# Full-height second score products in a three-layer fp32 network: 64-row matmuls replaced by 128-row ones over twice-stored low parts

## The chip, the cores and the metric

The kernel runs on one core of one Trainium2 chip. The metric is the device time of one execution in microseconds (us), lower is better. The engines are PE (TensorE, matmul; its weight loads are listed apart as PEld), DVE (VectorE), ACT (ScalarE), POOL (GpSimd) and SP (SyncE, whose queue issues nearly all DMAs).

## The reference

One sequence of 512 tokens with 1024 channels goes through three layers and a last norm, in float32:

```
layer 1: x += norm(w_out(gated sum of three mixers)):  gated linear attention (4 heads),
         sliding-window attention (8 heads of 64, 2 key heads), multi-scale pooling;  then a conv-FFN
layer 2: x += fox(x):   16 heads of 64;  scores q.k/8 plus a forgetting bias, causal softmax;  then a conv-FFN
layer 3: x += mla(x):   16 heads;  scores (q_nope.k_nope + q_rope.k_rope) / sqrt(192), 128 and 64 rows;
         the rotary key k_rope is one for all heads;  block-causal softmax;  then a conv-FFN
out = norm(x)
```

What matters here are the scores: products over 64 rows (the head's channels) in the sliding-window heads, in all fox heads, and in the rotary part of every mla head.

## The kernel before

**Two-part products.** To keep float32 accuracy with single-pass matmuls, every operand is kept as a pair of fp32r parts, a high and a low one. A product of two pairs is three matmuls into one PSUM bank (`mm3`): high by high, high by low, low by high. The large projections stream their weights from HBM (`raw` chunks of 512 KB on SP's queue, split into `hi` by ACT, L276, and `lo` by DVE, L277) and run with 512 token columns.

**Scores of 64-row heads.** Two heads with 64 rows each share a tile of 128 rows. `stack_q` (L423) makes a tile `Q` whose plane j holds, for head j, its high part in one half of the 128 rows and its low part in the other. `stack_k` (L432) makes `K`, whose plane j holds head j's high part twice, in both halves: ACT casts the key tile to `KH` (L437), four SBUF-to-SBUF DMAs on SP's queue (L440, 64 rows by 512 columns each, two per head) copy it, and DVE subtracts the rest to `KL` (L441), which stays where it is, one head in rows 0 to 63 and the other in rows 64 to 127. A score tile is then two matmuls (`mm_stacked`, L444): `Q` by `K` over all 128 rows, which gives (high + low of q) by (high of k), and a second one over the 64 rows of the head alone, high of q by low of k. In the profile these are `sc<-K,Q` and `sc<-KL,Q`, in the sliding-window part `swas<-K,Q` and `swas<-KL,Q`.

**Rotary part.** In `mla` the rotary key `kr` already stands in both halves of the rows, as a high and a low tile. A score tile there is three 128-row matmuls (`sc<-hl`), then `qr` by `kr[0]` over 128 rows, then `qr` by `kr[1]` over 64 rows (both are `sc<-hl,Q`).

**Each head** takes its four query blocks one after the other, with 128, 256, 384 and 512 key columns (sliding window: 128 and three times 256), two matmuls each (five in mla). So the matmuls of a head are a burst in which the 128-row and the 64-row form alternate. After the burst come the row maxima (DVE), exponentials (ACT), normalisation (ACT and POOL), ten transposes on PE (`t<-cst,pa` and the like), their split into `pth` (ACT) and `ptl` (DVE), and the product with the values (`fpo`, `mpo`).

**Order.** PE's order is fixed by the program. A head is a task whose steps go between the matmuls of the projections: after each step it says how many us of PE work, by a table of costs, are to pass before the next one (`LAG`; for example 22.08 between a fox head's scores and its transposes), and `mm` advances that clock by a cost per column that knows nothing of rows. The other engines' order is made by a list scheduler. All tiles come out of pools with a fixed number of buffers: `nslot` = 36 slots of 4 KB per partition, 9 of 2 KB (`t2`), 8 PSUM banks. In `fox` a pair of heads is begun by the projections `fq` and `fk`, `stack_q` and `stack_k`; there are eight pairs. The sliding-window part calls `stack_k` once.

Of the kernel before, what the change touches and what calls it, by code (L numbers as in the profile page):

```python
# [7 lines left out]
F32 = mybir.dt.float32  # L8
# [10 lines left out]
UPC = 8        # 128x128 units in one chunk of the weight stream  # L19
# [4 lines left out]
WHOLE = (6, 8, 7)     # output tiles that are not computed by halves of the tokens  # L24
LEVELS = (64, 32, 16, 8, 4, 2, 1)

# columns of the parameter array
# [12 lines left out]
# columns of the constant array  # L40
# [6 lines left out]
# columns of the array of narrow weights, and how many for each k  # L47
_NCOLS = {"glow": (0, 32), "fgt": (256, 32), "krope": (512, 64)}
NRES = 384     # columns that stay on chip
# [5 lines left out]
def tfk_plan():  # L55
    """The weight stream: one entry for each 128x128 unit, in the order of use."""
    plan = []

    def cols(name, k0, nk, c0, nn=1):
        while len(plan) % nn:  # L60
            plan.append(None)
        for k in range(nk):
            for n in range(nn):
                plan.append((name, k0 + k, c0 + n))

    for k in range(8):
        for n, t in FIRST:
            plan.append((n, k, t))
    cols("gv", 0, 8, 0, 4)
    cols("sv", 0, 8, 0)  # L70
    cols("sk", 0, 8, 0)
    for t in range(4):
        cols("sq", 0, 8, t)
    for t in range(4):
        cols("pu", 0, 8, t)
    for t in range(4):
        cols("gr", 0, 8, t)
    cols("poolw", 0, 4, 0)
    for br in "cba":
        for t in range(8):  # L80
            cols("gate_" + br, 0, 8, t)
            cols("br_" + br, 0, 4, t)
    def align():
        while len(plan) % UPC:
            plan.append(None)

    def grouped(name, k0, nk, tiles):
        for k in range(nk):
            for t in tiles:
                plan.append((name, k0 + k, t))  # L90

    grouped("wout", 0, 8, range(WOUT_WHOLE))
    align()
    for t in range(WOUT_WHOLE, 8):
        cols("wout", 0, 8, t)

    def ffn(i):
        tiles = [j * DFF_T + t for t in range(DFF_T) for j in range(2)]
        if i == 0:
            align()  # L100
            grouped("up0", 0, 8, tiles[:UP0_FIRST])
            tiles = tiles[UP0_FIRST:]
        for t in tiles:
            cols(f"up{i}", 0, 8, t)
        whole = WHOLE[i]
        for t in range(whole):
            cols(f"down{i}", 0, DFF_T, t)
        for _ in range(2):
            for t in range(whole, 8):
                cols(f"down{i}", 0, DFF_T, t)  # L110

    ffn(0)
    cols("fv", 0, 8, 0, 4)
    align()
    cols("fq", 0, 8, 0)
    cols("fv", 0, 8, 0, 4)
    cols("fv", 0, 8, 4, 4)
    for p in range(8):
        if p:
            cols("fq", 0, 8, p)  # L120
        cols("fk", 0, 8, p)
    grouped("fout", 0, 8, range(4))
    for t in range(4, 8):
        cols("fout", 0, 8, t)
    ffn(1)
    for t in range(2):
        cols("dkv", 0, 8, t)
    for t in range(6):
        cols("dq", 0, 8, t)

    def mout(g):
        for t in range(8):
            cols("mout", 4 * g, 4, t)

    def keys_values(p):
        for h in (2 * p, 2 * p + 1):
            cols("uk", 0, 2, h)
        for g in UV_AT.get(p, ()):
            cols("uv", 0, 2, 4 * g, 4)

    for p in range(8):
        if p == 0:
            keys_values(p)
        for t in (0, 2, 1):
            cols("uq", 0, 6, 3 * p + t)
        if p:
            keys_values(p)
        if p in MOUT_AFTER:
            mout(MOUT_AFTER[p])
    mout(3)  # L150
    ffn(2)
    align()
    return plan


def tfk_kept(e):
    """Whether the unit stays on chip for a second use."""
    return e and (e[0] == "wout" and e[2] >= WOUT_WHOLE or e[0] == "up0" and (e[2] % DFF_T) * 2 < UP0_FIRST
                  or e[0] == "fq" and e[2] == 0)
# [6 lines left out]
# the work of TensorE that goes between a step of a task and the next one, which needs its result  # L166
# [10 lines left out]
class Fut:  # L177
    """A value that a task in the background will set."""
# [17 lines left out]
class Net:  # L196
    def __init__(self, ctx, tc, xin, wall, par, cst, msk, nar, out, dbg=None):
# [8 lines left out]
        self.nslot, self.nt2 = 36, 9  # L206
# [29 lines left out]
    # ---- allocation  # L236
# [27 lines left out]
    # ---- the weight stream  # L264
# [33 lines left out]
    def narrow(self, name):  # L298
        """The weights of a product of few columns, by k: [high, low] of w columns each, as one operand."""
        nc, (c, w) = self.nc, _NCOLS[name]  # L300
        raw = self.slot([P, 8, w], F32, "nraw")
        hl = self.slot([P, 8, 2, w], F32R, "nhl")
        nc.sync.dma_start(out=raw, in_=self.nar[:, c:c + 8 * w].rearrange("p (k w) -> p k w", k=8))
        nc.scalar.copy(out=hl[:, :, 0], in_=raw)
        nc.vector.tensor_tensor(out=hl[:, :, 1], in0=raw, in1=hl[:, :, 0].bitcast(F32), op=ALU.subtract)
        return [hl[:, k].rearrange("p a w -> p (a w)") for k in range(8)]

    # ---- tasks whose products go between those of the projections
# [28 lines left out]
    # ---- products  # L337
# [14 lines left out]
    def proj(self, name, t, xs, k0=0, ps=None, cols=ALL):  # L352
        """out^T tile t of the product with the moving operands xs (pairs of high and low parts)."""
# [8 lines left out]
    def proj_narrow(self, ws, xs, ps=None, cols=ALL):  # L362
        """Two passes: the product has its parts in the rows from 0 and from w on."""
# [7 lines left out]
    def add_narrow(self, ps, w, n):  # L371
        """The sum of the parts of such a product, n rows of it."""
# [15 lines left out]
    def proj_halves(self, tiles, halves):  # L388
        """As proj_group, for moving operands whose halves of the tokens come one after the other."""
# [5 lines left out]
    def proj_tok(self, name, c0, xs, ms=range(4), pss=None):  # L395
        """Token-major product: tiles of [128 tokens, 512 columns]."""
# [13 lines left out]
    # ---- splitting  # L410
# [4 lines left out]
    def split_scaled(self, src, scale, out=None):  # L415
        """src * scale in two parts; scale is a number or a column."""
# [6 lines left out]
    def stack_q(self, q):  # L423
        """[[high; low], [low; high]] of two heads of 64 rows."""
# [7 lines left out]
    def stack_k(self, k):  # L432
        """[[high; high], [high; high]] of two heads of 64 rows, and [low; low] of both."""
        nc = self.nc
        K = self.slot([P, 2, T], F32R, "K")
        H, L = (self.t2(dt=F32R, name=n) for n in ("KH", "KL"))
        nc.scalar.copy(out=H, in_=k)  # L437
        for j in range(2):
            for r in range(2):
                nc.sync.dma_start(out=K[64 * r:64 * r + 64, j].bitcast(F32), in_=H[64 * j:64 * j + 64].bitcast(F32))  # L440
        nc.vector.tensor_tensor(out=L, in0=k, in1=H.bitcast(F32), op=ALU.subtract)  # L441
        return K, L

    def mm_stacked(self, out, Q, K, L, j, qs, ks, start=True):  # L444
        r = slice(64 * j, 64 * j + 64)
        self.mm(out, Q[:, j, qs], K[:, j, ks], start, False)
        self.mm(out, Q[r, j, qs], L[r, ks], False, True)
# [8 lines left out]
    # ---- norms  # L456
    def rsqrt(self, src, inv_d, w):
        """(src * inv_d + EPS) ** -0.5 for [128, w]"""
# [20 lines left out]
    def bcast(self, rs):  # L479
        """[128, n] by token -> PSUM [128, 128 n], the same in each partition."""  # L480
# [15 lines left out]
    def add_square(self, acc, src, eng=None, cols=ALL, first=False):  # L496
        """acc += src * src, in the given columns"""
# [23 lines left out]
    def x_start(self, nxt):  # L521
        """x gets new values; nxt names the gain that its next use has."""
# [6 lines left out]
    def x_ready(self, k, cols=ALL):  # L529
        """x tile k has its values in these columns: what the next part needs of it."""  # L530
# [24 lines left out]
    def normed(self, gain):  # L555
        """The parts of x * gain; the factor by token comes later, from stats."""
        return [self.split_scaled(self.xk(k), self.p(gain, k)) for k in range(8)]

    def log_sigmoid(self, z, b, shape, out):
        """out = log_sigmoid(z + b), z in PSUM or SBUF, b a column."""  # L560
# [13 lines left out]
    # ---- first layer  # L574
    def mixer(self, nxt):
# [13 lines left out]
        # gated linear attention  # L589
# [24 lines left out]
        # sliding window attention  # L614
# [18 lines left out]
        # pooling  # L633
# [168 lines left out]
    def swa(self, t, g, q, k, V, of, fut):  # L802
        """Head t + 4 g."""
# [87 lines left out]
    def post_norm(self, name, xs, gain, nxt, group, whole):  # L891
        """x += rmsnorm(product) * gain; the tiles from `whole` on go by halves of the tokens, so that
        the norm of the first half runs beside the products of the second."""
# [55 lines left out]
    def finish(self, h, sq):  # L949
        """The last norm, of half of the tokens."""  # L950
# [15 lines left out]
    # ---- feed-forward  # L966
# [30 lines left out]
    # ---- causal softmax attention, shared parts  # L997
    def soft(self, src, dst, mx):
        """dst[n] = softmax of src[n] along the keys."""
# [21 lines left out]
    def transpose_probs(self, p):  # L1021
        """[(high, low)] of the transposed weights by key block: [128 keys, 512 - 128 kb queries]"""
# [13 lines left out]
    # ---- forgetting attention  # L1036
    def fox(self, nxt):
# [33 lines left out]
        def bias(h):  # L1071
            """-cum of the keys, the same for each query, and with the mask of the block on the diagonal."""
# [53 lines left out]
    # ---- latent attention  # L1126
    def mla(self, nxt):
# [28 lines left out]
        def rope(src, scl, stack):  # L1156
            """[128, 512] of rows x1 x2 x1 x2 (32 each), src in PSUM or SBUF"""
# [24 lines left out]
        def head(h, qn, kn, qr, V, fut):  # L1182
            j = h % 2
            r = slice(64 * j, 64 * j + 64)
            sc = self.score_bank()
            mx = self.tiny([P, 4], F32, "mx")
            for n in range(4):
# [3 lines left out]
                self.mm(sc[n], qr[r, j, n * P:w], kr[1][r, 0:w], False, True)  # L1191
# [89 lines left out]
# ---- layout on the host  # L1281
# [106 lines left out]
```

## Time and profile before

| | |
|---|---|
| three runs | 2290.30, 2292.85, 2297.34 us; median 2292.85 |
| profiled execution, first to last instruction (span) | 2290.4 us, 2.4 us under the median |
| PE busy | 2254.1 us, 98% |
| DVE, ACT, POOL busy | 62%, 45%, 12% |
| DMA | 206.30 MB; q1, which SP feeds, 28.5% of the 16 engines |
| PE's share of the chain that ended last | 91% |

A span is the time between the first and the last instruction of the program; busy shares are averages over stages with different limits. PE's matmuls overlap each other and their ends are modelled, so a PE that is busy all the time need not be at its full rate: what one matmul costs is read from where the next one starts.

### The profile page before, as it was taken

The numbers are of one execution on the slowest core, as the hardware profiler recorded it, in microseconds if no ns is written. First come the engines' busy times: TensorE is split into PE (matmuls) and PEld (weight loads), VectorE is DVE, ScalarE is ACT, GpSimd is POOL, SyncE is SP. The second block draws the span as 40 slices with busy tenths as digits, with TensorE's granted clock in tenths as the row PEclk, the third lists the DMA queues.
The fourth block names the chain that finished last, engine by engine and source line by source line (L and its number), as shares of the span: only waits on it lengthen the run. The fifth ranks groups of instructions, "written<-read, shape, count | busy, mean of one in ns | idle before, by whom it ended". The sixth has DMA issues, their size and how long they took to land.

```text
span 2290.4 us, 27755 instructions
## 1 busy us (share of the span) xinstructions
PE 2254.1 (98%) x10664; PEld 1850.6 (81%) x10664; DVE 1421.2 (62%) x2349; ACT 1021.8 (45%) x1672; POOL 278.7 (12%) x231
## 2 busy tenths in 40 slices
PE   8999999999999998999999999999999999999998
PEld 6777888898888897777888888887788788888887
DVE  6778544578777248667677774357555556777623
ACT  4343322354444235566544443235645564444322
POOL 4211100030000004454200000002100101000000
PEclk9989999999999999999999999999999999999998
DMA  4200323332332343433233333332122212233323
GB/s 159 65 28 28 101 93 101 101 102 74 93 101 94 99 129 122 125 98 102 65 92 98 95 100 94 101 100 71 47 65 65 74 47 92 92 102 92 101 94 100
DMA packets 61956, 206.30 MB, mean 90 GB/s; under 512 B 7152, under 2 KB 9584, under 8 KB 61824
## 3 DMA queue, kind: packets, MB, share of 16 engines
q1 hardware_dynamic: 61392, 203.74, 28.5%
q8 instruction: 84, 1.38, 0.2%
q10 hardware_dynamic: 432, 0.79, 0.1%
q14 instruction: 48, 0.39, 0.1%
HBM read 197.65 MB, written 2.13 MB: 87 GB/s over the span
## 4 chain that ended last, share of the span: by engine, by line
PE 91%; DVE 5%; ACT 1%; issue 1%; DMA 1%; POOL 0%; SPq 0%; DVEq 0%; ACTq 0%; POOLq 0%
PE up L339 31%; PE down L339 14%; PE sc L339 5%; PE uq L339 4%; PE mout L339 4%; PE gate_a L339 2%; PE gate_b L339 2%; PE gate_c L339 2%; PE fq L339 2%; PE fout L339 2%; PE wout L339 2%; PE lev L339 2%; PE fk L339 2%; PE sq L339 1%; DVE xs L420 1%; PE mpo L339 1%
## 5 line engine op out<-in xcount | busy, mean ns | idle before, releaser
L277 DVE TENSOR_TENSOR lo<-raw,hi 128x1024 fp32r<-128x1024 f32 (+1 forms) x348 | 440.4, 1266 | 325.0 <-ACT hi L276 320.7
L339 PE MATMUL up<-xs,hi 128*128 128x512 f32 x2016 | 621.7, 390 | 0.0
L276 ACT CAST hi<-raw 128x1024 fp32r<-128x1024 f32 (+1 forms) x348 | 365.4, 1050 | 571.7 <-PE down L339 171.1
L339 PEld LDWEIGHTS up<-xs,hi 128*128 128x128 f32 x2016 | 378.2, 188 | 79.4 <-issue 1.0
L339 PE MATMUL up<-xs,lo 128*128 128x512 f32 x1008 | 392.2, 389 | 0.0
L339 PE MATMUL down<-hl,hi 128*128 128x512 f32 (+1 forms) x1188 | 332.7, 366 | 0.0
L339 PEld LDWEIGHTS down<-hl,hi 128*128 128x128 f32 x1188 | 214.8, 189 | 36.3
L339 PEld LDWEIGHTS up<-xs,lo 128*128 128x128 f32 x1008 | 189.2, 188 | 39.3
L339 PE MATMUL down<-hl,lo 128*128 128x512 f32 (+1 forms) x594 | 217.1, 365 | 0.0
L502 POOL TENSOR_TENSOR acc<-acc,sq 128x256 f32<-128x256 f32 (+1 forms) x48 | 56.2, 1170 | 771.3 <-ACT sq L499 769.7
L979 DVE TENSOR_TENSOR u<-up,rsb 128x512 f32<-128x512 f32 x132 | 90.2, 687 | 80.9 <-PE up L339 76.7
L981 ACT ACTIVATE c<-u,par 128x512 f32<-128x512 f32 x132 | 107.0, 814 | 60.1 <-DVE u L979 59.8
L339 PEld LDWEIGHTS down<-hl,lo 128*128 128x128 f32 x594 | 112.0, 189 | 18.0
L982 DVE SCALAR_TENSOR_TENSOR c<-u,par,c 128x511 f32<-128x511 f32 x132 | 98.5, 747 | 23.8 <-ACT c L981 23.7
L918 POOL TENSOR_TENSOR x<-x,yo 128x256 f32<-128x256 f32 x32 | 28.7, 933 | 608.6 <-DVE yo L917 608.6
L983 DVE SCALAR_TENSOR_TENSOR c<-u,par,c 128x510 f32<-128x510 f32 x132 | 98.9, 749 | 4.0
L339 PE MATMUL uq<-hl,hi 128*128 128x512 f32 x288 | 90.5, 395 | 1.4 <-POOL hl L453 1.4
L452 ACT CAST hl<-c 128x512 fp32r<-128x512 f32 x66 | 40.8, 618 | 104.6 <-DVE c L990 104.6
L339 PE MATMUL mout<-hl,hi 128*128 128x512 f32 x256 | 80.4, 395 | 0.0
L988 ACT ACTIVATE c<-c 128x512 f32<-128x512 f32 x66 | 41.6, 630 | 70.1 <-DVE c L983 70.0
L420 DVE SCALAR_TENSOR_TENSOR xs<-x,par,xs 128x512 fp32r<-128x512 f32 (+1 forms) x64 | 61.9, 1006 | 7.9 <-ACT xs L419 7.9
L339 PEld LDWEIGHTS uq<-hl,hi 128*128 128x128 f32 x288 | 53.2, 188 | 14.9 <-issue 2.2
(392 smaller groups left out, 3995.1 us busy)
## 6 DMA issues: line engine op xcount, KB each, us to landing
raw<-in_wall_dram SPq DMA_DIRECT2D x359, 512.0 KB, 3.5
K<-KH SPq DMA_DIRECT2D x36, 128.0 KB, 2.3
bias<-cumd SPq DMA_DIRECT2D x16, 256.0 KB, 4.0
out_dram<-x SPq DMA_DIRECT2D x8, 256.0 KB, 2.4
x<-in_x_dram SPq DMA_DIRECT2D x7, 256.0 KB, 5.4
raw<-in_wall_dram SPq DMA_DIRECT2D x2, 256.0 KB, 4.0
early<-in_cst_dram SPq DMA_DIRECT2D x1, 512.0 KB, 6.3
msk<-in_msk_dram SPq DMA_DIRECT2D x1, 512.0 KB, 6.5
```

The lines of the kernel that those rows point to most:

```text
L276: nc.scalar.copy(out=hi[:, c], in_=raw[:, c])
L277: nc.vector.tensor_tensor(out=lo[:, c], in0=raw[:, c], in1=hi[:, c].bitcast(F32), op=ALU.subtract)
L339: self.nc.tensor.matmul(out, lhsT=a, rhs=b, start=start, stop=stop)
L420: nc.vector.scalar_tensor_tensor(out=lo, in0=src, scalar=scale, in1=hi.bitcast(F32), op0=ALU.mult, op1=ALU.subtract)
L452: nc.scalar.copy(out=hi, in_=src)
L502: (eng or self.nc.vector).tensor_tensor(out=acc[:, cols], in0=acc[:, cols], in1=sq[:, cols], op=ALU.add)
L918: nc.gpsimd.tensor_tensor(out=x, in0=x, in1=yt, op=ALU.add)
L979: v.tensor_tensor(out=u, in0=ps, in1=rsb, op=ALU.mult)
L981: nc.scalar.activation(out=c, in_=u, func=AF.Identity, scale=self.p(conv, 88 + t), bias=self.p(conv, 132 + t))
L982: v.scalar_tensor_tensor(out=c[:, 1:], in0=u[:, 0:T - 1], scalar=self.p(conv, 44 + t), in1=c[:, 1:], op0=ALU.mult, op1=ALU.add)
L983: v.scalar_tensor_tensor(out=c[:, 2:], in0=u[:, 0:T - 2], scalar=self.p(conv, t), in1=c[:, 2:], op0=ALU.mult, op1=ALU.add)
L988: nc.scalar.activation(out=g, in_=g, func=func)
```

## The change

The second matmul of a score tile now spans all 128 rows. For this `stack_k` makes a second slot tile `L`, in which plane j holds head j's low part in both halves, by four more DMAs; so `Q` by `L` also adds the product of the two low parts, which was left out before. In `mla` the row slice is dropped from `qr` and `kr[1]`, whose rows stand there twice already. The slots go from 36 to 39; a parameter that reserves memory for DMA descriptors of the program is set to 1024 so that they fit. Comments and doc strings that the diff removes are left out here.

```diff
-        self.nslot, self.nt2 = 36, 9
+        self.nslot, self.nt2 = 39, 9
...
     def stack_k(self, k):
         nc = self.nc
-        K = self.slot([P, 2, T], F32R, "K")
-        H, L = (self.t2(dt=F32R, name=n) for n in ("KH", "KL"))
-        nc.scalar.copy(out=H, in_=k)
-        for j in range(2):
-            for r in range(2):
-                nc.sync.dma_start(out=K[64 * r:64 * r + 64, j].bitcast(F32), in_=H[64 * j:64 * j + 64].bitcast(F32))
-        nc.vector.tensor_tensor(out=L, in0=k, in1=H.bitcast(F32), op=ALU.subtract)
+        out = K, L = [self.slot([P, 2, T], F32R, n) for n in ("K", "L")]
+        parts = [self.t2(dt=F32R, name=n) for n in ("KH", "KL")]
+        nc.scalar.copy(out=parts[0], in_=k)
+        nc.vector.tensor_tensor(out=parts[1], in0=k, in1=parts[0].bitcast(F32), op=ALU.subtract)
+        for a, b in zip(out, parts):
+            for j in range(2):
+                for r in range(2):
+                    nc.sync.dma_start(out=a[64 * r:64 * r + 64, j].bitcast(F32), in_=b[64 * j:64 * j + 64].bitcast(F32))
         return K, L
 
-    def mm_stacked(self, out, Q, K, L, j, qs, ks, start=True):
-        r = slice(64 * j, 64 * j + 64)
-        self.mm(out, Q[:, j, qs], K[:, j, ks], start, False)
-        self.mm(out, Q[r, j, qs], L[r, ks], False, True)
+    def mm_stacked(self, out, Q, K, L, j, qs, ks):
+        self.mm(out, Q[:, j, qs], K[:, j, ks], True, False)
+        self.mm(out, Q[:, j, qs], L[:, j, ks], False, True)
...
             j = h % 2
-            r = slice(64 * j, 64 * j + 64)
...
                 self.mm(sc[n], qr[:, j, n * P:w], kr[0][:, 0:w], False, False)
-                self.mm(sc[n], qr[r, j, n * P:w], kr[1][r, 0:w], False, True)
+                self.mm(sc[n], qr[:, j, n * P:w], kr[1][:, 0:w], False, True)
...
-    nc = _bacc.Bacc("TRN2", target_bir_lowering=False, num_devices=1)
+    nc = _bacc.Bacc("TRN2", target_bir_lowering=False, num_devices=1, dynamic_dma_scratch_size=1024)
```

On PE, in the sliding-window part, the score burst of a head reads as follows (`swas` is the PSUM bank of the scores; the sizes are those of the output):

```order
 L339 MATMUL swas<-K,Q 128x128
-L339 MATMUL swas<-KL,Q 128x128
+L339 MATMUL swas<-L,Q 128x128
 L339 MATMUL swas<-K,Q 128x256
-L339 MATMUL swas<-KL,Q 128x256
+L339 MATMUL swas<-L,Q 128x256
 L339 MATMUL swas<-K,Q 128x256
-L339 MATMUL swas<-KL,Q 128x256
+L339 MATMUL swas<-L,Q 128x256
```

Nothing moves on PE, here and in the whole program: the same matmuls stand in the same places, and the second of each pair takes another tile.

On SP's queue, in `fox`, from the third pair of heads to the fifth, there stood (`raw` is the weight stream, `bias` a copy for the forgetting bias):

```order
L440 DMA K<-KH 64x512 x4
L1074 DMA bias<-cumd 128x512 x2
L275 DMA raw<-in_wall_dram 128x1024 x2
L440 DMA K<-KH 64x512 x4
L1074 DMA bias<-cumd 128x512 x2
L275 DMA raw<-in_wall_dram 128x1024 x2
L440 DMA K<-KH 64x512 x4
```

and now there stands:

```order
L442 DMA K<-KH 64x512 x4
L442 DMA L<-KL 64x512 x4
L1075 DMA bias<-cumd 128x512 x2
L275 DMA raw<-in_wall_dram 128x1024 x2
L442 DMA K<-KH 64x512 x4
L275 DMA raw<-in_wall_dram 128x1024
L442 DMA L<-KL 64x512 x4
L1075 DMA bias<-cumd 128x512 x2
L275 DMA raw<-in_wall_dram 128x1024
L442 DMA K<-KH 64x512 x4
L442 DMA L<-KL 64x512 x4
```

Four issues more for each pair, behind those of `K`; in the fourth pair a transfer of the weight stream has come between the two.

On ACT, in `fox`, ahead of the fifth pair's key cast, there stood (`pa` holds a head's probabilities, `pts` the split of its transposes):

```order
L276 CAST hi<-raw 128x1024
L437 CAST KH<-fk 128x512
L1010 ACTIVATE pa<-pa,den 128x128
L1010 ACTIVATE pa<-pa,den 128x384
L452 CAST pts<-t_8135 128x256
```

and now there stands:

```order
L276 CAST hi<-raw 128x1024
L1011 ACTIVATE pa<-pa,den 128x128
L1011 ACTIVATE pa<-pa,den 128x384
L437 CAST KH<-fk 128x512
L453 CAST pts<-t_8165 128x256
```

In this pair the cast that `K`'s copies wait for stands behind two normalisations. Outside `fox`, and one place in the sliding-window part, the other engines' orders are as before.

## Rows read from the trace of the kernel before

**Rows 1.** The page: PE's busy time; the chain that ended last, by engine.

```profile
PE 2254.1 (98%) x10664; PEld 1850.6 (81%) x10664; DVE 1421.2 (62%) x2349; ACT 1021.8 (45%) x1672; POOL 278.7 (12%) x231
...
PE 91%; DVE 5%; ACT 1%; issue 1%; DMA 1%; POOL 0%; SPq 0%; DVEq 0%; ACTq 0%; POOLq 0%
```

**Rows 2.** Timeline of PE, a fox head's scores: start us, us, instruction.

```profile
942.66 0.39 PE L339 MATMUL fk<-xs,lo 128*128 128x512 f32 x1
942.89 0.22 PE L339 MATMUL sc<-K,Q 128*128 128x128 f32 x1
943.04 0.33 PE L339 MATMUL sc<-KL,Q 64*128 64x128 f32 x1
943.29 0.38 PE L339 MATMUL sc<-K,Q 128*128 128x256 f32 x1
...
945.51 0.73 PE L339 MATMUL fk<-xs,hi 128*128 128x512 f32 x2
946.08 0.40 PE L339 MATMUL fk<-xs,lo 128*128 128x512 f32 x1
```

**Rows 3.** Timeline of PEld (weight loads), the same burst.

```profile
942.66 0.19 PEld L339 LDWEIGHTS sc<-K,Q 128*128 128x128 f32 x1
943.03 0.18 PEld L339 LDWEIGHTS sc<-KL,Q 64*128 64x128 f32 x1 [0.18 <-issue]
```

**Rows 4.** Timeline of PE, an mla head's scores.

```profile
1590.47 0.44 PE L339 MATMUL sc<-hl 128*128 128x128 f32 x3
1590.76 0.53 PE L339 MATMUL sc<-hl,Q 128*128 128x128 f32 x2
...
1595.02 0.73 PE L339 MATMUL uq<-hl,hi 128*128 128x512 f32 x2
1595.59 0.39 PE L339 MATMUL uq<-hl,lo 128*128 128x512 f32 x1
```

**Rows 5.** Timeline of PE, a fox head's product with the values.

```profile
1016.12 0.34 PE L339 MATMUL fpo<-pth,fV 128*128 128x384 f32 x1
1016.30 0.35 PE L339 MATMUL fpo<-ptl,fV 128*128 128x384 f32 x1
1016.49 0.40 PE L339 MATMUL fpo<-pts,fV 128*128 128x256 f32 x2
1016.72 0.22 PE L339 MATMUL fpo<-pth,fV 128*128 128x128 f32 x1
```

**Rows 6.** Timeline of PE, first and next row of a sliding-window head's burst.

```profile
109.12 0.33 PE L339 MATMUL swas<-K,Q 128*128 128x128 f32 x1
...
111.50 1.22 PE L339 MATMUL sq<-xs,hi 128*128 128x512 f32 x2
```

**Rows 7.** Timelines of ACT, SP and PE: key copies, first and last fox pair.

```profile
937.02 0.61 ACT L437 CAST KH<-fk 128x512 fp32r<-128x512 f32 x1
937.66 2.38 SPq L440 DMA_DIRECT2D K<-KH  x4
...
1080.86 0.61 ACT L437 CAST KH<-fk 128x512 fp32r<-128x512 f32 x1
1084.45 0.30 PE L339 MATMUL sc<-K,Q 128*128 128x128 f32 x1 [1.43 <-DVE ptl L453]
```

**Rows 8.** The page's DMA issues: count, KB each, median us to landing.

```profile
K<-KH SPq DMA_DIRECT2D x36, 128.0 KB, 2.3
```

**Rows 9.** Windows: us, busy us by engine, PE's granted clock, DMA share, GB/s.

```profile
118.30:132.00 13.70, 13.70 (x42) 10.44 (x43) 8.38 (x21) 5.29 (x13) 2.87 (x2) 0.50 0.00 0
1087.70:1091.10 3.40, 3.40 (x12) 2.96 (x11) 1.80 (x10) 1.70 (x6) 0.00 (x0) 0.50 0.00 0
940.00:1100.00 160.00, 157.71 (x713) 118.61 (x712) 108.39 (x348) 102.98 (x251) 77.93 (x59) 0.99 0.34 99
1590.00:1880.00 290.00, 290.00 (x1403) 232.59 (x1402) 158.38 (x325) 171.57 (x366) 29.67 (x23) 1.00 0.19 60
```

**Rows 10.** Waits of PE from 940 to 1100 us: total, times, longest.

```profile
PE fpo L339 <- DVE ptl L453: 0.9, 3, 0.4
```

## The prediction

> **What bounds the kernel now.** I read the page first: PE is busy for 98% of the span and holds 91% of the chain that ended last [rows 1], so time is won or lost where PE's next matmul starts earlier or later. A busy PE is no PE at its rate, so the second view is the timeline of PE through the scores of one head of each kind, where the distance from one start to the next is read, not the duration. What a matmul of full height costs stands beside it: 0.23 us with 512 columns (`fk` to the first `sc`) [rows 2], 0.18 with 384 and 0.115 with 256 [rows 5], 0.10 with 128 (three in 0.29) [rows 4].
>
> In a fox head's burst the starts are further apart than that. `K,Q` with 128 columns is followed after 0.15, and the 64-row one after it by the next full one after 0.25 us, though 0.10 of streaming is due. The loads show why: the first load of the burst starts 0.23 us ahead of its matmul, while the one before runs; the load for the 64-row matmul starts with its matmul, after 0.18 us in which PEld waited for nothing that the profile shows [rows 3]. At each change of height PE runs empty first. DVE, ACT and DMA are not what bounds these stretches now: from 940 to 1100 us DVE is busy 108.39 and ACT 102.98 of 160, in mla 158.38 and 171.57 of 290 [rows 9].
>
> **What it removes.** The eight fox products take 942.89 to 945.51, 2.62 us [rows 2]. At full height throughout they take two each of 0.10, 0.115, 0.18 and 0.23, that is 1.25: 1.37 less. The two `fk` after the burst take 0.57 where 0.46 is due [rows 2]; with that 0.11 a head saves 1.48, and 16 heads 23.7 us.
>
> An mla head's twenty products take 1590.47 to 1595.02, 4.55 us; five of each size at full rate are 3.13; with the same 0.11 after it (two `uq` in 0.57) a head saves 1.53 [rows 4], and 16 heads 24.6 us. Here the full-height form of this very operand is in the trace: `qr` by `kr[0]` follows `sc<-hl` without a gap, the 64-row one is what follows it.
>
> A sliding-window head takes 109.12 to 111.50, 2.38 us [rows 6]; two of 0.10 and six of 0.115 are 0.89: 1.49 each, 11.9 us for eight. The step behind the burst I leave out: some bursts stand beside 64-row products of the linear attention, where a change remains.
>
> Removed in sum: 23.7 + 24.6 + 11.9 = **60.2 us** of PE time, all of it on the chain. No product is added, moved or made wider, and a product of full height takes as long as its columns.
>
> **What it adds.** 36 more copies of 128 KB on SP's queue. Four issues take 2.38 us, 0.60 each [rows 7], and a copy lands 2.3 us after its issue [rows 8]. A first head needs plane 0 of `L`: issues five and six. So `L` is there 5 x 0.60 + 2.3 = 5.3 us after the first issue of `K`, which follows `KH`'s end at once (937.63, 937.66) [rows 7]; before, `KL` was ready with DVE's subtraction.
> - First pair: 937.66 + 5.3 = 942.96, and the second product is due at 942.89 + 0.10 [rows 2]: on time.
> - Last pair: `KH` ends at 1081.47, `L` lands at 1086.8, the product is due at 1084.55: 2.25 late. This pair shows the wait already: its first product waits 1.43 us [rows 7]. The profile names DVE, but `K`'s second copy lands at 1081.5 + 0.6 + 2.3 = 1084.4, so I take it for the copy.
> - The distance from `KH`'s end to the scores is 5.26 us in the first and 2.98 in the last pair. Between the two ends I take the mean, 1.13 us for each of eight: **9 us**, bounds 0 (all like the first) and 18 (all like the last; the pair whose `KH` now stands behind two normalisations, and the one with a `raw` transfer ahead of `L`, lean there). Second heads come later and lose nothing. The sliding-window part makes one `L`, and between its key projection and its first scores PE runs the 24 products of `sq`, 24 x 0.23 = 5.5 us, which covers the copies; if not, it costs 5.3 us once.
> - Behind `L` on SP stand `bias` and `raw`, 2.4 us later each pair. A pair takes some 20 us (160 by eight) [rows 9], of which `K` and `L` take 4.8 on SP, so the queue has room; were that cover gone, the `raw` delay would be PE's, 2.4 x 8 = 19 us, inside the next bound.
>
> The other cost is on the queues of DVE and ACT. In fox PE comes back to a head's value product when `ptl` is ready, and three times it waited already, 0.9 us in all [rows 10]. Heads without slack give back what their burst saves. Below, nothing; above, all of fox's 23.7. With three such heads shown I take four: 4 x 1.5 = **6 us**. In mla PE is busy for all 290.00 us, and DVE and ACT for under 60% [rows 9]; shortened by 24.6 of 290 they stay under 65%, so I count nothing.
>
> The DVE subtraction, the cast and the operand `Q` are as before. Three more slots issue nothing; `L` is held by them. The reserved memory is that of descriptors, and the program's DMAs stay on the same queues: nothing.
>
> **Sum.** 60.2 - 9 - 6 = 45 us. On the profiled span 2290.4 - 45 = 2245; on the median of the runs, 2.4 us above it, **2248 us**.
>
> **A rule that speaks against it.** In the trace a full-height load runs while a full-height matmul does: the load at 942.66 starts with `fk`, 0.23 us ahead of its product [rows 2, 3], and three full products of 128 columns follow each other in 0.29 [rows 4] though one load takes 0.19. The Trainium skill, "TensorE: Matmul & The Clock Gate", section on packing small matmuls, says that a weight load overlaps a running matmul only when their row groups differ. By that rule full-height products would each show their load. The trace does not agree, and I follow it.
>
> **Rivals.**
> - *Loads no longer hidden.* If the 160 second products each showed their 0.19 us load, 30 us of the 60 would be gone: 2248 + 30 = 2278. Against it: `sc<-hl` in rows 4. Chance 0.02.
> - *Fox becomes bound by DVE, ACT and the copies.* PE's fox stretch would shrink from 160 to 136 us, with DVE's 108 and POOL's 78 and chains between them. With both costs at their upper bounds, 18 + 23.7, time is 2293 - 60 + 41 = 2274. For it: the waits of rows 7 and 10 exist. Against it: most value products had no wait. Chance 0.16.
> - *The clock.* From 118.30 to 132.00 PE was granted 0.50, that is 1.2 in place of 2.4 GHz, in the sliding-window part, where the bursts stand; so also for 3.4 us from 1087.70, some 3 us behind the last fox pair's wait and scores [rows 7, 9]. A denser burst could spare the first: half of 13.7, 6.9 us, time 2241 (0.10). Waits of 2 us for `L` in every pair could bring the second eight times: 8 x 1.7, time 2262 (0.10).
> - *Slower.* `L` comes so late that its wait exceeds what the kernel saves: eight pairs would each have to wait 60/8 = 7.5 us. The place is SP's queue, where `L` stands behind a `raw` that waits for its buffer; but that order is in one pair of eight, and 2.25 us is what the last pair shows. At 9 us a pair: 2293 - 60 + 72 = 2305. Chance 0.02.
> - *It does nothing*, if the empty time came from the change of operand and not of height: 2293. Against it: `sc<-hl` to `hl,Q` at full height shows none. Chance 0.02.
>
> **How the numbers follow.** The forecast has 0.58, with a range of its own from 2238 (both costs a third) to 2257. The range for 8 in 10 goes from 2233 (no cost at all) to 2266, which leaves out about half of the fox rival, the small ones and some of the clock on either side. A difference under 0.3%, 7 us, is about what a measurement of this kernel cannot tell from none; faster by more than that 0.96, within 0.02, slower 0.02.
>
> **What would show it.** Right: in mla the burst takes 3.1 to 3.3 us in place of 4.55 and the stretch is 23 to 25 us shorter; in fox a burst whose `L` is there takes 1.3; a sliding-window burst 0.9. The copy: PE waits ahead of the second score product of fox's later pairs, 1 to 2.5 us. Wrong: starts in a burst that stay 0.2 us apart beyond their columns; PE waits for `pth`, `ptl` or PSUM in most fox heads; waits in mla; or half-clock stretches behind the new waits.

## The result and the profile after

| | before | after |
|---|---|---|
| runs, us | 2289.21 to 2297.34, median 2291.57 (4) | 2253.37 to 2258.01, median 2254.90 (4) |
| profiled span, us | 2290.4 | 2251.7 |

The ratio is 0.9838, with a 95% interval from 0.9815 to 0.9861: 36.7 us less, where the forecast was 45. The time lies in the range from 2233 to 2266, and under the 2274 of the rival in which fox is bound elsewhere; by stage the picture is another one, as the windows below show.

The page of the changed kernel, the two lines that answer to [rows 1]:

```profile
PE 2196.6 (98%) x10664; PEld 1837.5 (82%) x10664; DVE 1415.0 (63%) x2349; ACT 1020.5 (45%) x1672; POOL 279.2 (12%) x231
...
PE 85%; DVE 8%; ACT 3%; DMA 2%; issue 2%; SPq 1%; POOL 0%; DVEq 0%; ACTq 0%; POOLq 0%
```

PE executes the same 10664 matmuls in 57.5 us less busy time, but the span fell only by 38.7: the chain now runs through DVE, ACT and DMA for 13% in place of 7%.

Where the time went is read by stage. Each row is one window: us, then busy us (and count) of PE, PEld, DVE, ACT, POOL, then PE's mean granted clock, DMA share and GB/s. The first is the sliding-window part (first `swas` to last `pu`), the second fox (first `sc` to last `fout`), the third mla (first `sc` to last `mpo`). Before:

```profile
109.10:225.10 116.00, 115.79 (x553) 89.84 (x553) 88.82 (x224) 48.52 (x123) 19.11 (x17) 0.90 0.09 28
942.90:1144.20 201.30, 198.69 (x915) 152.70 (x914) 137.02 (x383) 124.74 (x287) 89.54 (x66) 0.99 0.32 93
1590.50:1885.40 294.90, 294.90 (x1429) 236.86 (x1427) 161.07 (x328) 172.71 (x368) 29.17 (x23) 1.00 0.19 58
```

After:

```profile
108.90:206.60 97.70, 95.26 (x554) 77.26 (x554) 89.66 (x224) 47.85 (x123) 20.45 (x17) 1.00 0.11 33
924.10:1128.30 204.20, 184.02 (x915) 153.06 (x914) 132.18 (x383) 124.73 (x287) 88.37 (x66) 0.96 0.41 113
1574.60:1846.40 271.80, 271.44 (x1428) 234.49 (x1427) 160.93 (x328) 172.09 (x368) 29.15 (x23) 1.00 0.22 63
976.90:983.70 6.80, 4.90 (x16) 4.02 (x16) 3.41 (x17) 0.34 (x2) 3.20 (x3) 0.50 0.48 119
1004.20:1007.60 3.40, 3.02 (x9) 2.76 (x10) 1.45 (x9) 0.00 (x0) 0.00 (x0) 0.51 0.91 211
1052.00:1055.40 3.40, 3.40 (x11) 2.81 (x10) 3.09 (x15) 1.23 (x2) 0.32 (x1) 0.50 0.69 188
1072.50:1075.90 3.40, 3.40 (x12) 2.99 (x11) 2.36 (x15) 0.86 (x4) 0.00 (x0) 0.50 0.39 145
```

The sliding-window part is 18.3 us shorter and mla 23.1; fox is 2.9 us *longer*. The rest of the program keeps its length within 1 us. In fox PE is busy for 14.7 us less, and stands idle for 20.2 in place of 2.6. Its granted clock fell from 0.99 to 0.96; the last four rows are the stretches at 1.2 GHz, 17.0 us in sum, where there was one of 3.4 [rows 9]. In the sliding-window part the clock went the other way, from 0.90 to 1.00.

The waits of PE after (total, times, longest), in fox, which answer to [rows 10], and below the dots the longest in the sliding-window part:

```profile
PE sc L339 <- DMA L<-KL: 14.1, 7, 5.3
PE sc L339 <- DMA K<-KH: 2.9, 2, 1.7
PE fpo L339 <- DVE ptl L454: 1.4, 4, 0.5
PE t L344 <- DVE mx L1096: 1.3, 1, 1.3
PE fout L339 <- DVE hl L454: 0.2, 1, 0.2
...
PE U L339 <- ACT kt L753: 1.9, 1, 1.9
```

The copies of the low parts are late in seven of eight pairs (all but the third). The timeline of PE after: a sliding-window burst (answers to [rows 6]), the late burst of the fourth pair, a fox burst whose `L` is there [rows 2], and an mla burst [rows 4]:

```profile
108.85 0.33 PE L339 MATMUL swas<-K,Q 128*128 128x128 f32 x1
...
109.89 0.63 PE L339 MATMUL sq<-xs,hi 128*128 128x512 f32 x2
...
973.16 0.22 PE L339 MATMUL sc<-K,Q 128*128 128x128 f32 x1
978.72 0.44 PE L339 MATMUL sc<-L,Q 128*128 128x128 f32 x1 [5.34 <-DMA L<-KL]
978.96 0.52 PE L339 MATMUL sc<-K,Q 128*128 128x256 f32 x1
...
985.87 0.22 PE L339 MATMUL sc<-K,Q 128*128 128x128 f32 x1
...
987.15 0.63 PE L339 MATMUL fk<-xs,hi 128*128 128x512 f32 x2
...
1574.59 0.45 PE L339 MATMUL sc<-hl 128*128 128x128 f32 x3
...
1577.78 0.62 PE L339 MATMUL uq<-hl,hi 128*128 128x512 f32 x2
```

The bursts now take 1.04, 1.28 and 3.19 us in place of 2.38, 2.62 and 4.55. The late one waits 5.34 us for `L` and then goes on at half clock: `sc<-L,Q` with 128 columns takes 0.24 to the next start. What it waited for stands on SP's timeline:

```profile
969.01 3.40 SPq L442 DMA_DIRECT2D K<-KH  x4
972.52 0.53 SPq L275 DMA_DIRECT2D raw<-in_wall_dram  x1
973.22 2.39 SPq L442 DMA_DIRECT2D L<-KL  x4
```

This is the pair in which the order puts a `raw` of 512 KB between `K` and `L`. The issue is 0.7 us behind that `raw`, and the copies land 4.9 us after issue, where the median over all 36 is 2.3; the view of the tile `L` says so:

```profile
DMA to landing us min/median/max: 2.2/2.3/4.9
```

### The profile page after: what moved, and what is told of

The parts are those of the page before. It is cut to its first block, busy times and chain, and to the rows that moved or that the text cites. A ratio compares the mean times of both kernels' runs of the same rounds, so it can differ in the third digit from the quotient of the medians.

```text
span 2251.7 us, 27823 instructions
## 1 busy us (share of the span) xinstructions
PE 2196.6 (98%) x10664; PEld 1837.5 (82%) x10664; DVE 1415.0 (63%) x2349; ACT 1020.5 (45%) x1672; POOL 279.2 (12%) x231
## 4 chain that ended last, share of the span: by engine, by line
PE 85%; DVE 8%; ACT 3%; DMA 2%; issue 2%; SPq 1%; POOL 0%; DVEq 0%; ACTq 0%; POOLq 0%
PE up L339 31%; PE down L339 15%; PE mout L339 4%; PE uq L339 3%; PE sc L339 3%; PE gate_a L339 2%; PE gate_b L339 2%; PE gate_c L339 2%; PE fout L339 2%; PE wout L339 2%; DVE lo L277 2%; PE lev L339 1%; DVE xs L420 1%; PE mpo L339 1%; PE dq L339 1%
```

## The experiments

The theory was that a change between 128-row and 64-row matmuls costs PE about 0.18 us, in the burst and behind it, and that what fox did not give comes from the copies of `L`. The rivals were that the 64-row product itself is dear wherever it stands, that fox is bound by DVE and ACT whatever the copies do, and that the sliding-window gain comes from other things than its bursts. Where a row of windows stands below, it is over the same stretch as above.

**e1_mla**: before, with the last product of mla alone at full height.

```diff
-                self.mm(sc[n], qr[r, j, n * P:w], kr[1][r, 0:w], False, True)
+                self.mm(sc[n], qr[:, j, n * P:w], kr[1][:, 0:w], False, True)
```

> The kernel before with the last product of mla's scores alone at full height; no copies, no other edit. Theory (each change between 128 and 64 rows costs time, and in mla nothing else waits): the mla stretch, from the first score to the last value product, goes from 294.9 to about 272 us, all other stretches stay, the time is about 2269 us, 23 less. Rival (mla's gain is a shift that other engines give back later): the feed-forward behind mla gets longer and the time falls by under 15 us. In the sliding-window part the three half-clock stretches (24 us in sum) should still be there.

Measured: 2271.48 us (2257.60 to 2277.17, 4 runs) against 2290.93, ratio 0.9917 [0.9894, 0.9941]. In the trace mla went from 294.9 to 271.9 us, and fox is about as long as before (199.6). The window of mla:

```profile
1579.30:1851.20 271.90, 271.50 (x1428) 234.48 (x1427) 160.90 (x328) 172.31 (x368) 29.23 (x23) 1.00 0.21 63
```

But the profiled run is the lowest of the four, and its sliding-window part, where nothing was edited, is 9.3 us shorter:

```profile
109.10:215.80 106.70, 106.49 (x554) 82.69 (x553) 89.63 (x224) 48.25 (x123) 19.13 (x17) 0.98 0.10 31
```

Its clock there is 0.98 in place of 0.90: one stretch of 3.4 us at half clock, not 23.9 us of them. That part of the expectation missed. These stretches come and go between runs of one kernel: the mean granted clock of this run is 0.995, that of the other three 0.985 to 0.989.

**e4_group**: before, with mla's products in another order: the full-height ones of blocks 1 to 3, then the 64-row ones of all blocks together, then the full-height ones of block 0. Every product is there; a head has two changes of height, not eight. `full` issues a block's four full-height products, `part` its 64-row one.

```diff
+            for n in (1, 2, 3):
+                full(n, True, False)
+            for n in (1, 2, 3):
+                part(n, False, True)
+            part(0, True, False)
+            full(0, False, True)
```

> The kernel before with mla's score products in another order and none of them changed in height: full-height products of blocks 1 to 3, then their 64-row ones and block 0's, then block 0's full-height ones, so that a head changes height twice and not eight times. Theory (the cost sits in the changes): six of eight changes go, 16 heads x 1.5 x 6/8 = 18 us less in mla, time about 2274. Rival (a 64-row product is slow by itself, whatever stands beside it): mla stays at 295 us and the time at 2291.

Measured: 2278.16 us (2275.69 to 2284.41), ratio 0.9942 [0.9922, 0.9962]. The window of mla, and the new wait in it:

```profile
1591.30:1872.90 281.60, 277.81 (x1429) 233.16 (x1427) 160.25 (x328) 171.57 (x368) 29.54 (x23) 1.00 0.20 61
```

```profile
PE t L344 <- DVE ptl L453: 3.8, 4, 1.3
```

PE's busy time fell by 294.90 - 277.81 = 17.1 us with all 64-row products still there, 1.07 a head; full height takes 294.90 - 271.44 = 23.5, or 1.47 a head. Six of eight changes gone gave 73% of it. The cost sits in the change, not in the 64-row product. 3.8 us came back as a wait of the transposes. A shorter burst alone doesn't bring that wait, since with the still shorter bursts of e1 and of the changed kernel it is 0.3 us; that the new order of the blocks does is not shown.

**e3_nocopy**: before, with all second products at full height over `KL` as it lies, so that the other head's low parts are multiplied in too; no copies, no `L`.

```diff
-        self.mm(out, Q[r, j, qs], L[r, ks], False, True)
+        self.mm(out, Q[:, j, qs], L[:, ks], False, True)
...
-                self.mm(sc[n], qr[r, j, n * P:w], kr[1][r, 0:w], False, True)
+                self.mm(sc[n], qr[:, j, n * P:w], kr[1][:, 0:w], False, True)
```

> The kernel before with all second products at full height and no copies: the second product takes KL as it lies, so that the other head's low part is multiplied by the low part of q and the high part by the wrong rows; the scores are off by that, the work on PE is that of the changed kernel. Theory (late copies cost fox 17 us of waits and some half-clock stretches that follow them): fox is 20 to 25 us shorter than in the changed kernel, the time 2231 to 2238 us. Rival (fox is held by DVE and ACT): fox stays at 195 to 204 us and the time at 2246 to 2255.

Measured: 2230.45 us (2229.22 to 2231.08), ratio 0.9729 [0.9715, 0.9744], a little under the forecast. Fox:

```profile
924.40:1105.80 181.40, 174.98 (x915) 147.47 (x914) 138.54 (x383) 124.11 (x287) 90.84 (x66) 1.00 0.35 103
```

Without the copies PE is busy in fox for 174.98 us, 23.7 less than before, idle for 6.4 and at full clock throughout. The copies of `L` cost the changed kernel 204.2 - 181.4 = 22.8 us of fox, nearly all that the shorter bursts give there. DVE and ACT do the same work in both, so they don't bind fox at 204. The three slots and the reserved memory go with the copies in every run, so no run tells their share.

**e2_copies**: the changed kernel's copies, slots and reserved memory, with 64-row second products everywhere.

```diff
+        r = slice(64 * j, 64 * j + 64)
-        self.mm(out, Q[:, j, qs], L[:, j, ks], False, True)
+        self.mm(out, Q[r, j, qs], L[r, j, ks], False, True)
...
-                self.mm(sc[n], qr[:, j, n * P:w], kr[1][:, 0:w], False, True)
+                self.mm(sc[n], qr[r, j, n * P:w], kr[1][r, 0:w], False, True)
```

> The changed kernel's copies of the low parts, its 39 slots and its reserved memory, but every second product over 64 rows again, as before. Theory (fox loses because the copies land late): PE waits some 10 to 17 us for L in fox, nothing else changes, and the time is 2301 to 2308 us, slower than before. Rival (fox loses because DVE and ACT become its bound once PE is faster): with PE as slow as before there is little wait for L, and the time is 2290 to 2296.

Measured: 2309.47 us (2304.63 to 2312.93), ratio 1.0073 [1.0053, 1.0094]: the copies by themselves make the kernel slower, by 18.5 us. Fox, and PE's waits in it:

```profile
945.50:1163.80 218.30, 207.17 (x915) 157.22 (x914) 137.13 (x383) 125.52 (x287) 90.84 (x66) 0.95 0.38 105
```

```profile
PE sc L339 <- DMA L<-KL: 7.7, 5, 3.5
PE sc L339 <- DMA K<-KH: 1.4, 1, 1.4
```

Of the 17.0 us that fox is longer, half is idle time (11.1 in place of 2.6) and half is PE busy for longer with the same work (207.17 to 198.69), at a clock of 0.95. The waits for `L`, 7.7 us, are under the 10 to 17 that were expected, and the time is 1.5 us above the expected range: what the theory left out is the clock, in this trace 20.4 us of fox at 0.50, where before had 3.4.

**e8_swa**: before, with full height over `KL` as it lies in the sliding-window part alone (`whole` sets the row slice of the second product to all 128 rows).

```diff
-            self.mm_stacked(out, q, *k, g, slice(n * P, (n + 1) * P), keys)
+            self.mm_stacked(out, q, *k, g, slice(n * P, (n + 1) * P), keys, whole=True)
```

> The kernel before with the second products at full height in the sliding-window part alone, and there without copies: KL as it lies, so that the other head's low part enters the scores; fox and mla as before. Theory (the bursts' changes of height cost 12 us there, and with them go the three half-clock stretches that cost 7 more): that part falls from 116 to 98 us in the profile, the time by 16 to 20 us to about 2273, with no half clock before 480 us. Rival (the half-clock stretches have nothing to do with the bursts): they stay, that part is 104 us, the time 2279.

Measured: 2272.13 us (2269.70 to 2278.72) against 2294.94, ratio 0.9912 [0.9886, 0.9939]. The window of the edited part:

```profile
108.20:205.80 97.60, 95.21 (x553) 77.20 (x553) 89.65 (x224) 47.90 (x123) 20.53 (x17) 1.00 0.11 33
```

All that this part gained comes with this one edit (97.60 beside the 97.70 above), and the clock is 1.00. The time fell by 22.8 us, a little more than the 16 to 20 expected. The rival, which left the half-clock stretches where they were (104 us), fell.

**e5_zero**: full height without copies of the low parts. `L` is one of three standing tiles that POOL fills with zeros once; DVE writes head j's low part into plane j, on the head's own rows. The other half multiplies by zero, so the sums are those of the kernel before. The edit is shown against the kernel before, with cuts at the dots.

```diff
+        self.low, self.nlow = [self.cpool.tile([P, 2, T], F32R, name=f"low{i}") for i in range(3)], 0
+        for t in self.low:
+            nc.gpsimd.memset(t.bitcast(F32), 0.0)
...
+        L = self.low[self.nlow % 3]
...
-        nc.vector.tensor_tensor(out=L, in0=k, in1=H.bitcast(F32), op=ALU.subtract)
+        for j in range(2):
+            r = slice(64 * j, 64 * j + 64)
+            nc.vector.tensor_tensor(out=L[r, j], in0=k[r], in1=H[r].bitcast(F32), op=ALU.subtract)
```

> The same full-height second products without copies of the low parts: L is one of three standing tiles that POOL fills with zeros once at the start; DVE subtracts head j's low part into plane j, rows of head j, by two 64-row subtractions in place of one of 128 rows, and the other half stays zero, so that the product is the one of the kernel before. 36 slots. Theory (only the late copies cost fox its gain): fox 181 to 186 us as without copies, sliding-window part 98, mla 272; 2230 to 2237 us. Rival (DVE's extra subtraction, some 0.6 us a pair ahead of the scores, or the write into a standing tile makes a new wait): PE waits for L from DVE in several pairs, fox above 192, time above 2243.

> The kernel with standing zero-padded low parts again, beside the one before it on the same chip: 2229 to 2233 us.

Measured: 2230.70 us (2229.71 to 2232.27) against 2294.94, ratio 0.9729 [0.9703, 0.9754]; in the second row of runs (e5_again) 2232.24 (2230.19 to 2235.04, 5 runs) against 2299.78, 0.9724 [0.9702, 0.9746]. It beats both kernels (its interval lies below the changed kernel's) and equals e3. Fox in the first, and PE's waits there:

```profile
922.90:1105.70 182.80, 176.00 (x914) 148.73 (x913) 141.60 (x390) 124.42 (x287) 89.72 (x66) 0.99 0.35 102
```

```profile
PE sc L342 <- DMA K<-KH: 3.9, 2, 2.1
PE fpo L342 <- DVE ptl L459: 2.6, 4, 1.4
```

The two subtractions of 64 rows in place of one add 4.6 us to DVE's busy time in fox (137.02 before, 141.60 now) and cost nothing visible.

**e6_planes**: the changed kernel with plane 0 of `K` and `L` copied ahead of plane 1, so that a first head needs the first four copies, not six.

```diff
-        for a, b in zip(out, parts):
-            for j in range(2):
+        for j in range(2):
+            for a, b in zip(out, parts):
```

> The changed kernel with its copies written plane by plane; in the order that comes out, the first L copies of most pairs stand behind three K copies in place of four. Theory (a pair's wait is the place of L's second copy on SP's queue, 0.6 us an issue): about 0.6 us less wait in each of the seven pairs that wait, PE's waits for L fall from 14 to 9 or 10 us, time 2249 to 2252. Rival (the wait is DVE's late KL or the landing time under traffic): waits for L stay at 13 to 15 us, time 2255.

Measured: 2251.06 us (2247.65 to 2253.22), ratio 0.9814 [0.9791, 0.9837]. The interval overlaps the changed kernel's, so no gain is settled. PE's waits in fox:

```profile
PE sc L339 <- DMA L<-KL: 8.6, 6, 4.1
PE sc L339 <- DMA K<-KH: 6.9, 3, 4.3
```

The waits for `L` fell by 5.5 us, a little more than expected, and the time lies in the expected range; but 4.0 us more go to waits for `K`, which the expectation had left out. The longest two waits, 4.1 and 4.3 us, are for copies that stand close behind a `raw` on SP's timeline:

```profile
974.60 1.01 SPq L275 DMA_DIRECT2D raw<-in_wall_dram  x1
975.78 2.40 SPq L442 DMA_DIRECT2D L<-KL  x4
```

```profile
992.96 9.13 SPq L275 DMA_DIRECT2D raw<-in_wall_dram  x2
1002.20 1.10 SPq L442 DMA_DIRECT2D K<-KH  x2
```

These copies landed 4.8 to 5.0 us after issue. So more than half of the waiting that is left (8.4 of 15.5 us) is for copies that stand behind a weight transfer; whether the order of the planes by itself gains something was not separated from that.

**e7_lag**: the changed kernel with the scores put later by the table.

```diff
-    "fox": 6.04,
+    "fox": 8.5,
```

> The changed kernel with one number of the table of lags altered: the first scores of a fox pair stand 2.46 us of PE work later (8.5 for 6.04). Theory (L is late by about 2 us for the scores, and nothing else holds fox): waits for L fall from 14 to under 4 us, fox from 204 to 188 to 192, time 2238 to 2244. Rival (later scores only move the wait to the transposes or the value products, because DVE and ACT set the pace): waits for ptl and the maxima rise by as much and the time stays above 2249.

Measured: 2245.16 us (2243.80 to 2246.21), ratio 0.9790 [0.9768, 0.9811], an interval just below the changed kernel's. Fox, and PE's five largest waits in it:

```profile
925.50:1118.80 193.30, 180.18 (x902) 152.71 (x901) 133.17 (x382) 124.87 (x285) 88.62 (x65) 0.96 0.41 117
```

```profile
PE fpo L339 <- ACT pth L453: 2.7, 2, 1.4
PE fpo L339 <- DVE ptl L454: 2.5, 3, 1.4
PE t L344 <- DVE ptl L454: 2.4, 2, 2.2
PE t L344 <- DVE pts L454: 2.3, 1, 2.3
PE fout L339 <- ACT hl L453: 2.1, 1, 2.1
```

No wait for `L` is left; fox is 10.9 us shorter (193.3), but idle time is still 13.1 us, now where heads meet DVE and ACT, and there are five stretches of 3.4 us at half clock, each beside one of these waits (1.3 to 2.3 us long). The trace lacks a few instructions of this stretch (902 matmuls of 915), so these sums are rough. The time lies between what the theory (2238 to 2244) and its rival (above 2249) gave, and each holds in part: the delay buys the copies time, and in its place PE waits for the softmax.

**e9_direct**: e5 with `K` cast straight into its own rows by two casts of 64 rows and only the other half copied: two copies, no `KH`.

```diff
-        nc.scalar.copy(out=H, in_=k)
...
+            nc.scalar.copy(out=K[r, j], in_=k[r])
+            nc.sync.dma_start(out=K[o, j].bitcast(F32), in_=K[r, j].bitcast(F32))
```

> The kernel with standing zero-padded low parts, and K's high parts written by two ACT casts of 64 rows straight into their own rows, so that two copies in place of four are left, plane 0's the first on the queue; KH goes. Theory (the waits that fox has left are for K's second copy): the wait for K, 3.9 us in two places, falls under 1.5, fox from 182.8 to about 180 us, time 2227 to 2230. Rival (the 0.6 us that ACT casts more in each pair delay the probabilities): waits for pth and ptl grow by as much, time 2230 to 2234.

Measured: 2237.90 us (2234.45 to 2241.94) against 2299.78, ratio 0.9746 [0.9722, 0.9770]; e5 beside it on the same chip had 2232.24. The theory fell: half the copies, and PE waits longer for them; fox takes 186.5 us where 180 was expected, and the time lies above both ranges. PE's waits in fox, and SP's timeline at the longest:

```profile
PE sc L342 <- DMA K<-K: 6.3, 2, 3.5
```

```profile
988.80 0.33 SPq L278 DMA_DIRECT2D raw<-in_wall_dram  x1
989.23 1.11 SPq L443 DMA_DIRECT2D K<-K  x2
```

The copies now stand 0.43 us behind a `raw`, and landed 4.9 and 4.8 us after issue, as those of the late pair above. The rival, that the longer casts delay the value products, isn't seen either: waits of `fpo` for `ptl` are 1.6 us, under e5's 2.6.

## Why the prediction was right, and where its terms were off

By its own steps; "measured" is from the windows and waits above.

| term | forecast, us | measured, us |
|---|---|---|
| mla bursts | -24.6 | -23.1 |
| fox bursts | -23.7 | -23.7 (PE busy, e3 against before; some 1.7 of it is clock) |
| sliding window, bursts | -11.9 | -9.7 (an estimate, below) |
| sliding window, clock and one wait | 0 (rival: -6.9) | -8.6 (the rest of -18.3) |
| copies of `L` late | +9 | +15.6 |
| queues of DVE and ACT | +6 | +1.8 |
| PE busy for longer than in e3, fox | 0 (rival: half clock, +13.6) | +9.0, of which some 7.4 is half clock |
| sum | -45 | -38.7, as the span fell |

**Bursts.** Right in mechanism, and in size within 1.5 us in mla and 1.7 in fox. e4 shows that the cost goes with the changes of height, and e1 that mla's share is gained without any other edit: 23.5 us over 16 heads of eight changes is 0.18 us for each change. The Trainium skill, "TensorEngine Tiling (Array Packing)", section Key Properties, says that a change of the tiling mode drains TensorE; if going from 128 to 64 rows is such a change, e4 agrees, with 17.1 us less for six of eight changes. Nothing of the rival of loads that are no longer hidden appeared. The rule behind it (the Trainium skill, "TensorE: Matmul & The Clock Gate", section on packing small matmuls: a load overlaps a matmul only if the row groups differ) is not what full-height bursts show: eight products take 1.28 us, and by 0.23 us for 512 columns their 2560 columns alone are 1.15, which leaves 0.13 for eight loads of 0.19. One reading of the prediction goes too far here: a product of 128 columns, 0.10 us from start to start, takes longer than its columns, which by the same figure are 0.06. Its sums use the 0.10 and stand.

**Sliding window.** The term of 11.9 us was a little large, and what was left out of the sum is the clock; the first half of that rival came true. The e1 run gives its price: this part is there as before, with 3.4 us at half clock in place of 23.9, and PE is busy for 9.3 us less (115.79 to 106.49), some 0.45 for each us. By this estimate 10.8 of the 20.5 us by which PE is busy for less (115.79 to 95.26) are clock, and 9.7 are left for the bursts, where eight times the 1.34 that the first one gave would be 10.7. PE now stands idle for 2.2 us more, 1.9 of it once for `kt` of the linear attention beside it. In the traces of the kernels with full-height bursts there (after, e3, e5, e5_again, e6, e7, e8, e9) no such stretch lies in this part; with alternating ones there are 23.9 us of them before, 30.7 in e2, 20.5 in e4 and 3.4 in e1. So the stretches come with the alternating bursts, but their number also changes by itself, and a run of the kernel before with few of them would show less of this gain. What in the bursts lowers the clock stays open.

**Copies.** Mis-sized, within the bounds (0 to 18). Forecast was a wait of 0 to 2.25 us in each pair. Six of the seven waits are of that size, 0.3 to 2.3; the seventh is 5.34, and takes a third of the total. The prediction named that pair as one that leans to the upper end, but took landing after 2.3 us for it too; behind the `raw` it was 4.9, and `L`'s first issue came 4.2 us after `K`'s first (969.01 to 973.22), not 2.4. The 15.6 are 14.1 for `L`, and 2.9 for `K` less the 1.43 that the last pair waited before [rows 7].

**Queues.** Four waits of `fpo`, as many as assumed, but of 0.35 us in the mean and not 1.5: PE reaches the value products later when it has waited for `L`, which is the likely reason. The 1.8 are these 1.4 and one wait of the transposes for `mx`, 1.3, less the 0.9 of before. Where the copies are gone or waited out (e5, e7), these waits grow to 2.6 and beyond 5 us. The cost exists, but the copies covered it.

**Clock in fox.** The second half of the clock rival: not eight stretches but 17.0 us in four places, each beside a wait of 2.0 to 5.3 us for `L`. It has no place in the sum of the forecast. Against e3 PE is busy for 9.0 us more (184.02 to 174.98). In the four stretches PE was busy for 14.7 us (the four rows above), half of which, 7.4, is what the same work would have saved at full clock; where the other 1.6 went stays open. That the waits bring the lower clock is argued and not shown: it goes with them in after, e2 and e6, but waits of 1.9 us in e3 and of 2.8 in e9 had no such stretch beside them, and in e2 and e4, where the bursts alternate, one of 3.4 us stands in fox beside no wait above 0.6.

That the result lies only 7 us from the forecast owes something to errors of both signs: 6.4 more in the sliding window and 4.2 less on the queues, against 6.6 more on the copies, 9.0 of longer busy time in fox and 1.5 less in mla. The total was right, and fox was not: there the terms come to 23.7 - 9 - 6, that is 8.7 us less, and the stretch became 2.9 us longer, on the way to the 18.0 more of the rival in which fox is bound by the copies and the queues. What made up for it is the clock in the sliding-window part, which stood among the rivals and not in the sum. So far the total is luck.

## What to carry to other kernels

Where matmuls of 64 and of 128 rows alternate in a burst, read the starts, not the busy time: each change of height cost some 0.18 us here, and it was gained back by filling the missing rows with zeros that are written once (e5), or for the larger part by grouping the products of one height (e4). Copies that make the full height possible are work on a queue with a latency; put the distance from their source to their use beside the issue times, and look for a large transfer just ahead of them. A wait can cost more than its length where PE's clock is lower beside it, as it was in fox.

## What the runs showed of the hardware that was not expected

- A copy of 128 KB within SBUF lands 2.3 us after issue in the median, but later behind a weight transfer of 512 KB on the same queue: of twelve that were issued within 1.3 us of one (in after, e2, e6, e7 and e9), eleven landed after 4.4 to 5.0 us and one after 3.1. Some landed late without one: the first three copies of `K` in the fourth pair after took 3.4 to 3.6. Whether the queue or the shared engines hold them up was not tried.
- PE busy for all of a stretch does not mean a full clock: with alternating heights it was granted 0.50 in 23.9 us of the sliding-window part with PE busy nearly throughout, and with full-height bursts nowhere there.
- The half-clock stretches differ between runs of one kernel: the one in fox starts at 1049.4 us in e5 and at 1032.2 in e5_again, and the four runs of e1, with mean clocks from 0.985 to 0.995, spread over 19.6 us, while those of e3 spread over 1.9. Why a run has few or many of them stays open.
